# A planner that orders a decoder trunk's instructions: VectorE and GpSimd exclude each other in the plan, and the search over orders moves urgencies in one stretch of time

## The chip, the core and the metric

The kernel runs on one core of a Trainium2 chip. A core has TensorE (PE: matmuls; PEld in the profile is its weight load), VectorE (DVE), ScalarE (ACT), GpSimd (POOL) and SyncE (SP), which issues the DMAs here. Each engine works through its own list of instructions in order and waits at semaphores for the others. SBUF is the on-chip memory, PSUM holds what matmuls produce. The metric is the device time of one execution in microseconds (us).

## The reference

Two layers of a decoder over 528 positions (16 learned ones and 512 of the input) of width 1024, batch 1, all in float32. Each layer:

```python
xn = rmsnorm(h, norm_mix_g[l])
z_ret, z_hgrn, z_rwkv, z_s5 = split_cols(xn @ w_in[l], ...)
o_ret = retention_mixer(z_ret, pos)        # chunkwise retention with rotary positions
o_hgrn = hgrn2_mixer(z_hgrn, ...)          # gated linear recurrence
o_rwkv, v_first = rwkv7_mixer(z_rwkv, ...) # generalised delta rule, position by position
o_s5 = s5_mixer(z_s5, ...)                 # complex diagonal state space, associative scan
h = h + concatenate([o_ret, o_hgrn, o_rwkv, o_s5]) @ w_out[l]
hn = rmsnorm(h, norm_ffn_g[l])
h = h + square(relu(hn @ w_ffn_up[l])) @ w_ffn_down[l]   # 1024 -> 4096 -> 1024
```

A final rmsnorm follows, and the 512 positions of the input are returned.

## The kernel before, in words

Activations lie with features on the 128 partitions and positions along the free axis, in two halves of 272 and 256 columns (one of 512 in the last layer). A large product takes three matmuls: weights and activations are each split into a high and a low part (ScalarE rounds the high part `wh` from the raw weights `wr`, VectorE subtracts to get the low part `wl`), and high by high, high by low and low by high are summed in PSUM. These are the names `bpi` (input projection), `bpo` (output projection), `bpu` and `bpd` (MLP up and down). Weights come in 256 KB loads `wr` through SP's queue into three raw buffers.

The four mixers run as many small matmuls with work on VectorE, ScalarE and GpSimd between them, among the matmuls of the input projection and, at their end, of the output projection. In the S5 mixer two scans on VectorE give `Irs` and `Iis` (real and imaginary part); then `Xrs` is Irs times a table less `t2s`, and `t2s`, Iis times a table, is computed on GpSimd. In the retention mixer the rotary positions are a product on VectorE (`rkz` times `csr`), a product on GpSimd (`rksz` times `csr`), and their sum on VectorE. The chain of rwkv goes through three segments of 192 positions (`re`, `rm`, `rf`), with round trips through DRAM (`sa`, `sd`).

None of this order is written out by hand. The class `Sched` records every instruction (`record`, L108), prices it (`price`), and `flush` (L250) plans a whole stretch of the program: the first flush comes in the middle of layer 0's MLP, the second in the middle of layer 1's MLP, the third at the end. `run` (L138) is a list scheduler: it keeps a clock for each engine, takes at each step the engine that is free first, and of its ready instructions the one with the lowest key (its urgency). It models PSUM banks, the tiling of TensorE, SP's queue, and puts matmuls on zeros (named `z`, issued at L303) into waits of TensorE that it foresees, which keeps that engine active. On every other engine an instruction takes its price whatever the other engines do:

```python
            else:
                z=clk[e]=t+c
```

`flush` plans many times and keeps the order whose last instruction ends first by the plan. It starts from the program's order, goes back and forth through the graph for 10 turns, and then disturbs all keys of the best order so far with random numbers of spread 1 us, 30 times, with 3 plans each. The third flush has no such search. The best order is fixed by dependencies without semaphores between neighbours on an engine; all instructions are recorded under L304.

Of the kernel before, what the change touches and what calls it, by code (L numbers as in the profile page):

```python
# [6 lines left out]
T=528; NM=16; PADT=48; TP=576  # L7
# [39 lines left out]
    pass  # L47

# [1 line left out]
STEP=1; WARM=6500.0; LEAST=3500.0; SWITCH=.1; DRAIN=.05; KEEP=3.0; WCOLS=256; WCOST=.112; WSAFE=.4; FLB=2; NPRE=3; TURNS=10; SHAKES=30; SHAKE=1.0; BANKS=8; CLASS=dict(hv='a',rw='a',hg='a',mx='a'); OWN=dict(a=3)  # L50
class _Engine:

    def __init__(s,eng,name,sched): s.eng=eng; s.name=name; s.sched=sched
# [3 lines left out]
        return g  # L57

class _Op:
    __slots__=("e","op","f","a","k","deps","pre","cost","succ","ready","cols","nbytes","chain","label","pri","order","mode","at","opens","banks")  # L60

TICK=10.24/3
def _box(x):
# [14 lines left out]
def _meet(a,b):  # L78
    if a[0]>b[1] or b[0]>a[1]: return False
    if a[2] is None or b[2] is None: return True  # L80
    return all(p<=w and v<=q for (p,q),(v,w) in zip(a[2],b[2]))
# [6 lines left out]
class Sched:  # L88
# [19 lines left out]
    def record(s,e,op,f,a,k):  # L108
        o=_Op(); o.e=e; o.op=op; o.mode=o.at=None; o.f=f; o.a=a; o.k=k; o.succ=[]; o.cols=o.nbytes=0; o.ready=0.0; o.chain=None; o.label=s.label; o.pri=s.pri
        if s.pri is not None: s.pri+=1  # L110
        out=k["out"] if "out" in k else a[0]
        ins=[x for x in list(a)+list(k.values()) if hasattr(x,"tensor") and x is not out]
        n=1
        for d in out.shape[1:]: n*=d
        price(o,out,ins,n)
        i=len(s.ops); deps=set()
        if op=="matmul":
            t=(out.tensor.name,out.offset)
            if k.get("start"): s.first[t]=i
            else: o.chain=s.first.get(t)  # L120
        if op=="matmul" and not k.get("start") or op=="copy_predicated": ins.append(out)
        for x,w in [(y,0) for y in ins]+[(out,1)]:
            t=x.tensor.name
            b=(0,1<<40,((0,1<<40),)) if t in s.psum else _box(x)
            W=s.wr.setdefault(t,[]); R=s.rd.setdefault(t,[])
            for c,j in W:
                if j!=i and _meet(b,c): deps.add(j)
            if w:
                for c,j in R:
                    if j!=i and _meet(b,c): deps.add(j)  # L130
                s.wr[t]=[(c,j) for c,j in W if not _within(c,b)]+[(b,i)]
                s.rd[t]=[(c,j) for c,j in R if j==i or not _within(c,b)]
            else: R.append((b,i))
            u=s.users.setdefault(t,[])
            if not u or u[-1]!=i: u.append(i)
            o.ready=max(o.ready,s.done.get(t,0.0))
        o.deps=deps; o.order=s.after-deps; s.ops.append(o)
    def run(s,key,back=False):  # L138


        ops=s.ops; N=len(ops)
        clk={e:0.0 for e in s.clk} if back else dict(s.clk); hw,dma=(0.0,0.0) if back else s.queue; mode,place=s.tiling; recent=collections.deque(s.recent); act=sum(x for _,x in recent); idle=[None]*N
        ready={e:[] for e in clk}; late={e:[] for e in clk}
# [1 line left out]
        push=heapq.heappush; pop=heapq.heappop  # L145

        free=sorted(s.banks); due=[]; use=dict(s.count) if not back else {}; place_={}; spare=BANKS-sum(OWN.values()); own=dict.fromkeys(OWN,0); extra=0
        line={c:0 for c in OWN}; dirty={}
        def can(i,t):

            v=ops[i].opens
# [9 lines left out]
        while todo:  # L161
            t=1e18
            for x in clk:
                p=late[x]; r=ready[x]
                while p and p[0][0]<=clk[x]:
                    i=pop(p)[1]; push(r,(key[i],i))
# [7 lines left out]
            while p and p[0][0]<=t:  # L174
                i=pop(p)[1]; push(r,(key[i],i))
            if e=="tensor" and not back:
                while due and due[0][0]<=t:
                    z,b,c=pop(due); push(free,(z,b))
# [6 lines left out]
            else:  # L185


                x=min(r_)
# [3 lines left out]
                o=ops[x[1]]  # L192
# [4 lines left out]
                i=x[1]; o=ops[i]; c=o.cost  # L197

                if o.mode!=mode: c+=SWITCH+(DRAIN if place is not None else 0.0); dirty={}
                if o.opens is not None:  # L200
                    x=min((y for y in free if y[0]<=t and not (o.mode[0]<128 and y[1] in dirty)),default=None) or free[0]
# [6 lines left out]
                if s.idle is not None:  # L208
                    K,M=[max(x,64) for x in o.mode]; p=clk[e]; w=WCOLS*K/128.0; d=WCOST if K==M==128 else WCOST/2+.002; fill=[]
                    x=sorted(y for y in free if y[0]+WSAFE<=p)  # L210
                    if K==128: x=[y[1] for y in x[:1]]
                    else:
                        z=[[y[1] for y in x if y[1]%2==q] for q in (0,1)]
                        x=[z[0][0],z[1][0]] if z[0] and z[1] and len(x)>3 else []
# [15 lines left out]
                mode=o.mode; place=o.at  # L230
                recent.append((t,o.cols)); act+=o.cols
            T[i]=t
            if o.nbytes:
                clk[e]=t+.06
                if back: hw=max(hw,t)+max(o.cost,o.nbytes/360e3); z=hw+.65
                else: hw=max(hw,t)+o.cost; z=dma=max(dma,hw+(.784 if e=="scalar" else .65))+o.nbytes/360e3
            else:
                z=clk[e]=t+c
            Z[i]=z
            if not back:  # L240
                for v in o.banks:
# [8 lines left out]
    def flush(s,turns=0):  # L250
        ops=s.ops

        last={}
        for (pn,tag),(bufs,names) in s.tags.items(): last.setdefault(pn,[]).extend(names[-bufs:])
        for (pn,tag),(bufs,names) in s.tags.items():
            for q,t in enumerate(names):
                if t not in s.users: continue
                if q>=bufs: before=[names[q-bufs]]
                else: before=last.get(pn-1,[]) if isinstance(pn,int) else []
                mine=set(s.users[t]); old=set(i for x in before for i in s.users.get(x,[])); at=max([s.done.get(x,0.0) for x in before],default=0.0)  # L260
                for i in s.users[t]:
                    if not ops[i].deps&mine: ops[i].deps|=old; ops[i].ready=max(ops[i].ready,at)
        s.count={}; s.queue_={c:[] for c in OWN}; s.until={}
        for i,o in enumerate(ops):
            o.opens=None; o.banks=sorted({x.tensor.name for x in list(o.a)+list(o.k.values()) if hasattr(x,"tensor")}&s.psum)
            for v in o.banks:
                if v not in s.count: s.count[v]=0; o.opens=v; s.queue_[s.tag[v]].append(v)
                s.count[v]+=1
        for o in ops: o.pre=[(j,lat(ops[j],o)) for j in o.deps]+[(j,-1e9) for j in o.order]
        for i,o in enumerate(ops):  # L270
            for j,l in o.pre: ops[j].succ.append((i,l))
        chain=lambda x: [o.pri-1e9 if o.pri is not None else x[i if o.chain is None else o.chain] for i,o in enumerate(ops)]
        best=None; key=list(range(len(ops))); keys=[key]
        def attempt(key,n):
            nonlocal best
            for it in range(n):
                if it: key=chain([-z for z in s.run([-z for z in Z],True)[1]])
                T,Z,state=s.run(key); m=max(Z)
                if best is None or m<max(best[1]): best=T,Z,state; keys[0]=key
        attempt(key,1)  # L280
        if turns:
            best=None; attempt(chain([-z for z in s.run([-z for z in s.run(key)[1]],True)[1]]),turns)

            rnd=random.Random(1)
            for _ in range(SHAKES):
                m=max(best[1]); key=[x+rnd.gauss(0.0,SHAKE) for x in keys[0]]; attempt(chain(key),3)
        T,Z,(s.clk,s.queue,s.tiling,s.recent,s.banks,idle,where)=best
        for t in s.users: s.done[t]=max(Z[i] for i in s.users[t])
        real={}
        def ap(x):  # L290
            if not hasattr(x,"tensor") or x.tensor.name not in s.psum: return x
            n=x.tensor.name
            if n not in real:
                b=where[n][0]; real[n]=s.pool.tile([128,512],F32,name="b"+n,tag=f"b{b}",bufs=1).tensor; s.now[b]=n
            return bass.AP(real[n],x.offset,x.ap)
        def issue(e,x):
            if e in s.prev: s.tc.add_manual_dep(x.ins,s.prev[e].ins.name,mybir.DependencyInfo(mybir.DependencyClass.NoSync,mybir.DependencyReason.DATA),reason="order")
            s.prev[e]=x
        for t,i in sorted((t,i) for i,t in enumerate(T)):
            o=ops[i]  # L300
            for b,K,M,p,q in idle[i] or ():
                if not hasattr(s.now[b],"tensor"): s.now[b]=s.pool.tile([128,512],F32,name=f"z{b}",tag=f"b{b}",bufs=1)
                issue("tensor",s.nc.tensor.matmul(s.now[b][q:q+M,:WCOLS],s.idle[p:p+K,:M],s.idle[p:p+K,:WCOLS],start=True,stop=True))  # L303
            issue(o.e,o.f(*[ap(x) for x in o.a],**{k:ap(x) for k,x in o.k.items()}))  # L304
        s.start()
# [891 lines left out]
def build(tc,A,o_ap):  # L1197
# [4 lines left out]
    with tc.tile_pool(name="kp",bufs=1) as kp, tc.tile_pool(name="ps",bufs=1,space=bass.MemoryType.PSUM) as pp:  # L1202
# [13 lines left out]
        class Weights:  # L1216
# [20 lines left out]
            def take(s,n=2):  # L1237
                while s.n<s.at+3: s.ahead()
                j=s.at; s.at+=n
                return j  # L1240
        def heavy(w,xs,n0,n1,nm,m=128,order=range(8),step=STEP,last=False):

# [402 lines left out]
```

## Time and profile before

| what | us |
|---|---|
| median of 3 runs | 1519.39 |
| lowest and highest of the 3 | 1514.93, 1519.92 |
| profiled execution | 1513.31 |
| its span, first to last instruction | 1511.5 |

The profiled execution's time is 1.8 us more than its span. Busy time of an engine is the time in which at least one of its instructions runs. Matmuls overlap (a matmul of 272 columns is listed with some 0.29 us, and the next starts about 0.12 us later), so TensorE's busy time also covers moments in which it works below its rate. A wait is listed with the engine and tile that ended it.

### The profile page before, as it was taken

How to read it: one execution, taken by the hardware profiler on the slowest of the kernel's cores; microseconds unless marked ns; L12 is line 12 of the kernel's file. 1: busy time of each engine (PE TensorE's matmuls, PEld its weight loads, DVE VectorE, ACT ScalarE, POOL GpSimd, SP SyncE). 2: the span in 40 equal slices, each digit the busy share in tenths (PEclk: the TensorE clock that was granted, in tenths of full speed). 3: DMA queues.
4: the chain of work that ended last, by engine and by line, in shares of the span. 5: the costliest groups of instructions: out<-in, count | busy, mean ns of one | idle time of the engine just before them, and what ended most of it. 6: DMA issues, size and time to landing. Idle time of an engine off the chain costs nothing.

```text
span 1511.5 us, 30536 instructions
## 1 busy us (share of the span) xinstructions
PE 1468.0 (97%) x11696; PEld 1334.1 (88%) x11696; DVE 922.2 (61%) x2237; ACT 582.1 (39%) x1163; POOL 428.2 (28%) x577
## 2 busy tenths in 40 slices
PE   9999998999999999999999999988999999999998
PEld 8988898779999999999999988987788888888887
DVE  8967888797833338333656756887957333333345
ACT  4443324632632423324434424246325323232342
POOL 3512673443323235332001100233311222222210
PEclk9999999999999999999999999999999999999999
DMA  5542345422222224323446624455112332322332
GB/s 175 176 141 74 102 136 158 132 58 71 91 92 85 98 85 136 112 85 95 131 136 209 178 55 116 132 164 173 57 63 92 97 98 91 98 93 96 98 105 77
DMA packets 143298, 168.54 MB, mean 112 GB/s; under 512 B 52144, under 2 KB 77168, under 8 KB 143152
## 3 DMA queue, kind: packets, MB, share of 16 engines
q1 hardware_dynamic: 143152, 166.59, 36.1%
q8 instruction: 92, 1.51, 0.4%
q14 instruction: 54, 0.44, 0.1%
HBM read 138.65 MB, written 27.56 MB: 110 GB/s over the span
## 4 chain that ended last, share of the span: by engine, by line
PE 75%; DVE 11%; DMA 5%; issue 4%; ACT 2%; SPq 1%; POOL 1%; POOLq 0%; DVEq 0%; ACTq 0%
PE bpd_v L304 24%; PE bpu_v L304 23%; PE bpi_v L304 10%; PE bpo_v L304 6%; PE z L303 2%; DVE wl L304 1%; SPq L304 1%; DMA wr<-in_win 1%; POOL t2s L304 1%; DMA sa<-Gm_L1c 0%; DVE Irs L304 0%; DMA vfv01c<-zdv 0%; PE bpor0c_v L304 0%; DMA csr1c<-in_cs 0%; DVE tms L304 0%
## 5 line engine op out<-in xcount | busy, mean ns | idle before, releaser
L304 ACT ACTIVATE wh<-wr 128x512 fp32r<-128x512 f32 (+1 forms) x388 | 243.5, 628 | 545.3 <-PE bpd_v L304 220.9
L304 DVE TENSOR_TENSOR wl<-wr,wh 128x512 fp32r<-128x512 f32 (+1 forms) x388 | 269.1, 695 | 280.2 <-ACT wh L304 277.5
L304 PE MATMUL bpi_v<-xha,wh 128*128 128x272 f32 (+2 forms) x864 | 253.8, 295 | 1.1 <-DVE ht_L1c L304 0.9
L304 PE MATMUL bpi_v<-xha,wl 128*128 128x272 f32 (+2 forms) x864 | 248.8, 289 | 3.2 <-DVE wl L304 3.2
L304 PE MATMUL bpi_v<-xla,wh 128*128 128x272 f32 (+2 forms) x864 | 247.2, 287 | 0.0
L304 PE MATMUL bpu_v<-xhf,wl 128*128 128x272 f32 (+2 forms) x768 | 246.7, 321 | 0.5 <-DVE wl L304 0.5
L304 PE MATMUL bpu_v<-xhf,wh 128*128 128x272 f32 (+2 forms) x768 | 247.0, 322 | 0.0
L304 PE MATMUL bpu_v<-xlf,wh 128*128 128x272 f32 (+2 forms) x768 | 245.4, 320 | 0.0
L304 PE MATMUL bpd_v<-xhh,wh 128*128 128x256 f32 (+2 forms) x736 | 233.8, 318 | 0.0
L304 PE MATMUL bpd_v<-xhh,wl 128*128 128x272 f32 (+2 forms) x736 | 233.6, 318 | 0.0
L304 PE MATMUL bpd_v<-xlh,wh 128*128 128x256 f32 (+2 forms) x736 | 232.5, 317 | 0.0
L304 POOL TENSOR_TENSOR xlh<-fs,xhh 128x272 fp32r<-128x272 f32 (+2 forms) x96 | 94.3, 982 | 309.9 <-DVE fs L304 236.0
L304 PEld LDWEIGHTS bpi_v<-xha,wh 128*128 128x128 f32 (+1 forms) x864 | 161.3, 187 | 5.7 <-DVE ht_L1c L304 1.2
L304 PEld LDWEIGHTS bpi_v<-xha,wl 128*128 128x128 f32 (+1 forms) x864 | 160.9, 187 | 5.5 <-DVE wl L304 4.1
L304 PEld LDWEIGHTS bpi_v<-xla,wh 128*128 128x128 f32 (+1 forms) x864 | 161.0, 186 | 1.0 <-issue 0.3
L304 PEld LDWEIGHTS bpu_v<-xhf,wl 128*128 128x128 f32 x768 | 144.5, 188 | 12.0 <-DVE wl L304 0.7
L304 PEld LDWEIGHTS bpu_v<-xlf,wh 128*128 128x128 f32 x768 | 144.5, 188 | 11.4
L304 PEld LDWEIGHTS bpu_v<-xhf,wh 128*128 128x128 f32 x768 | 144.6, 188 | 10.7
L304 PEld LDWEIGHTS bpd_v<-xlh,wh 128*128 128x128 f32 x736 | 138.3, 188 | 10.0
L304 PEld LDWEIGHTS bpd_v<-xhh,wl 128*128 128x128 f32 x736 | 138.3, 188 | 9.9
L304 PEld LDWEIGHTS bpd_v<-xhh,wh 128*128 128x128 f32 x736 | 138.4, 188 | 9.3
L304 POOL TENSOR_TENSOR h<-h,fd 128x272 f32<-128x272 f32 (+2 forms) x72 | 86.9, 1207 | 184.7 <-DVE fd L304 184.7
(922 smaller groups left out, 2534.3 us busy)
## 6 DMA issues: line engine op xcount, KB each, us to landing
wr<-in_wup SPq DMA_DIRECT2D x128, 256.0 KB
wr<-in_wdn SPq DMA_DIRECT2D x128, 256.0 KB
wr<-in_win SPq DMA_DIRECT2D x104, 256.0 KB
wr<-in_wout SPq DMA_DIRECT2D x32, 256.0 KB
h<-in_x SPq DMA_DIRECT2D x16, 264.0 KB
hD<-h SPq DMA_DIRECT2D x8, 264.0 KB
h<-hD SPq DMA_DIRECT2D x8, 264.0 KB
out<-out SPq DMA_DIRECT2D x8, 256.0 KB
```

The costliest lines, as they stand in the source:

```text
L303: issue("tensor",s.nc.tensor.matmul(s.now[b][q:q+M,:WCOLS],s.idle[p:p+K,:M],s.idle[p:p+K,:WCOLS],start=True,stop=True))
L304: issue(o.e,o.f(*[ap(x) for x in o.a],**{k:ap(x) for k,x in o.k.items()}))
```

## The change

Three things. `record` marks each instruction that uses the path shared by VectorE and GpSimd (`port`): every GpSimd instruction but memset; on VectorE those with two inputs in SBUF, and tensor_scalar and copies with an input in SBUF. `run` keeps three times in `held`: the end of VectorE's last marked instruction, and start and end of GpSimd's hold. A marked VectorE instruction that would start within GpSimd's hold starts at the hold's end. A marked GpSimd instruction has 0.33 us of its own (POOLUP), then takes the path at the end of VectorE's marked instruction. And `flush` makes 150 attempts in place of 30: the first 30 as before, 120 more with one plan each, in which only keys of instructions that start within one random stretch of 10 to 120 us are disturbed, by a spread of 0.3, 1 or 3 us; half of them start from keys taken from the plan backwards.

```diff
-STEP=1; WARM=6500.0; LEAST=3500.0; SWITCH=.1; DRAIN=.05; KEEP=3.0; WCOLS=256; WCOST=.112; WSAFE=.4; FLB=2; NPRE=3; TURNS=10; SHAKES=30; SHAKE=1.0; BANKS=8; CLASS=dict(hv='a',rw='a',hg='a',mx='a'); OWN=dict(a=3)
+STEP=1; WARM=6500.0; LEAST=3500.0; SWITCH=.1; DRAIN=.05; KEEP=3.0; WCOLS=256; WCOST=.112; WSAFE=.4; FLB=2; NPRE=3; TURNS=10; SHAKES=150; SHAKE=1.0; BANKS=8; POOLUP=.33; CLASS=dict(hv='a',rw='a',hg='a',mx='a'); OWN=dict(a=3)
...
         price(o,out,ins,n)
+
+        sb=sum(str(x.space).endswith("SB") for x in ins)
+        o.port=e=="gpsimd" and op!="memset" or e=="vector" and (sb>1 or sb and op in ("tensor_scalar","tensor_copy"))
...
-        line={c:0 for c in OWN}; dirty={}
+        line={c:0 for c in OWN}; dirty={}; held=[0.0]*3
...
             else:
-                z=clk[e]=t+c
+                if not o.port or back: z=t+c
+                elif e=="vector": z=held[0]=(held[2] if held[1]<=t<held[2] else t)+c
+                else: x=min(POOLUP,c); held[1]=max(t+x,held[0]); z=held[2]=held[1]+c-x
+                clk[e]=z
...
             rnd=random.Random(1)
-            for _ in range(SHAKES):
-                m=max(best[1]); key=[x+rnd.gauss(0.0,SHAKE) for x in keys[0]]; attempt(chain(key),3)
+            for it in range(SHAKES):
+                if it<30: key=[x+rnd.gauss(0.0,SHAKE) for x in keys[0]]; attempt(chain(key),3); continue
+                T,Z,_=best; m=max(Z); w=rnd.uniform(10.0,120.0); a=rnd.uniform(min(T)-w,m); d=rnd.choice((.3,1.0,3.0)); k=keys[0]
+                if rnd.random()<.5: k=chain([-z for z in s.run([-z for z in Z],True)[1]])
+                attempt([x+rnd.gauss(0.0,d) if a<=T[i]<=a+w and ops[i].pri is None else x for i,x in enumerate(k)],1)
```

The lists of instructions change order on every engine in the first two flushes. In the changed program the helper's lines are L312 (matmuls on zeros) and L313. Three lists follow, from two places.

VectorE, layer 0, second half of S5 (`01` in the names), before: the scans, then Irs and Xis times their table, the low part of a weight tile (`wl52`), a product of hgrn (`Kh0c0`), and the update of Xrs with GpSimd's t2s.

```order
L304 TENSOR_TENSOR Xrs01_626<-Irs01_621,Ps01_618 128x4x132
L304 SCALAR_TENSOR_TENSOR Iis01_622<-s5m4_370,Jis01_624 128x132
L304 TENSOR_TENSOR Irs01_621<-Irs01_621,Ps01_618 128x528
L304 TENSOR_TENSOR Xis01_627<-Iis01_622,Ps01_618 128x4x132
L304 COPY_PREDICATED hA160_526<-cst_62,blv1h0c0_v178_4239 16x32
L304 TENSOR_TENSOR wl52_321<-wr52_315,wh52_320 128x512
L304 TENSOR_TENSOR Kh0c0_534<-Kh0c0_534,tth0c0_537 128x4x4
L304 TENSOR_TENSOR Xrs01_626<-Xrs01_626,t2s01_628 128x4x132
```

The same place of the changed program.

```order
L313 TENSOR_TENSOR Xrs01_626<-Irs01_621,Ps01_618 128x4x132
L313 SCALAR_TENSOR_TENSOR Iis01_622<-s5m4_370,Jis01_624 128x132 x2
L313 TENSOR_TENSOR Irs01_621<-Irs01_621,Ps01_618 128x528
L313 TENSOR_TENSOR Xis01_627<-Iis01_622,Ps01_618 128x4x132
L313 TENSOR_TENSOR Xrs01_626<-Xrs01_626,t2s01_628 128x4x132
```

The weight tile's low part and the hgrn product no longer stand between Xis and the update of Xrs.

TensorE at the same place, before: the end of a projection (`bpi0_50`), a level of hgrn (`blv4`), then S5's output (`bs5y0s01`, of whose three matmuls for a group the one from Us needs no scan).

```order
L304 MATMUL bpi0_50_128_272_v54_4309<-xla7_95,wh51_317 128x256
L304 MATMUL bpi0_50_128_272_v54_4309<-xha7_94,wl51_318 128x256
L304 MATMUL blv4h0c0_v181_4344<-hB160_527,Kh0c0_534 16x16 x2
L304 MATMUL bs5y0s01_v229_4249<-Xrs01_626,CTs01_613 128x132
L304 MATMUL bs5y0s01_v229_4249<-Xis01_627,CTs01_613 128x132
```

The same place of the changed program.

```order
L313 MATMUL bpi0_50_128_272_v54_4331<-xla7_95,wh51_317 128x256
L313 MATMUL bpi0_50_128_272_v54_4331<-xha7_94,wl51_318 128x256
L313 MATMUL bs5y0s01_v229_4386<-Us01_620,M1s01_615 128x132
L313 MATMUL bs5y2s01_v230_4389<-Us01_620,M1s01_615 128x132
L313 MATMUL bpi0_52_128_0_v55_4393<-xha0_80,wh52_320 128x272
L313 MATMUL bpi0_52_128_0_v55_4393<-xla0_81,wh52_320 128x272
L313 MATMUL bs5y0s01_v229_4386<-Xrs01_626,CTs01_613 128x132
```

Two matmuls from Us and two of the next projection now stand ahead of the first use of Xrs.

TensorE in layer 1, at the transposes `btmkr1c1` of the retention keys `rkz`, before: behind a bonus term of rwkv, hgrn's diagonal and first level (`blv1`), with fills.

```order
L304 MATMUL bpb1L1c6_v616_15041<-bo_L1c6_8956,cst_62 128x192
L304 MATMUL bdgh1c2_v657_15044<-cst_62,QKh1c2_9022 128x2
L304 MATMUL blv1h1c2_v656_15048<-hB1281_8987,Kh1c2_9020 128x128 x2
L303 LDWEIGHTS zero_65
L303 MATMUL z2_15052<-zero_65 128x256
L303 LDWEIGHTS zero_65
L303 MATMUL z2_15052<-zero_65 128x256
L304 MATMUL blv1h1c2_v656_15048<-hB1281_8987,Kh1c2_9020 128x128
L304 MATMUL btmkr1c1_v696_15058<-cst_62,rkz1c1_9080 128x128 x3
```

The same place of the changed program.

```order
L313 MATMUL blv1h1c2_v656_15080<-hB1281_9007,Kh1c2_9040 128x128 x4
L313 MATMUL bzp2L1c6_v632_15089<-tav_L1c6_8979,tbk_L1c6_8980 64x64
L313 MATMUL bpo12L1c6_v634_15093<-SL1c0_8897,rav_L1c6_8967 64x64
L313 MATMUL bpo02L1c6_v633_15096<-SL1c0_8897,rav_L1c6_8967 64x64
L313 MATMUL bpo12L1c6_v634_15093<-tav_L1c6_8979,Gm_L1c6_8971 64x64
L313 MATMUL bpo02L1c6_v633_15096<-tav_L1c6_8979,Gm_L1c6_8971 64x64
L313 MATMUL bpo02L1c6_v633_15096<-SL1c0_8897,rav_L1c6_8967 64x64
L313 MATMUL bpo12L1c6_v634_15093<-SL1c0_8897,rav_L1c6_8967 64x64
L313 MATMUL bpo02L1c6_v633_15096<-tav_L1c6_8979,Gm_L1c6_8971 64x64
L313 MATMUL bpo12L1c6_v634_15093<-tav_L1c6_8979,Gm_L1c6_8971 64x64
L313 MATMUL bzp2L1c6_v632_15089<-tav_L1c6_8979,tbk_L1c6_8980 64x64 x3
L313 MATMUL btmkr1c1_v696_15115<-cst_62,rkz1c1_9100 128x128 x4
```

Twelve small matmuls of the rwkv chain now stand between hgrn's first level and the transposes.

## Rows read from the trace of the kernel before

**Rows 1.** The page: span, engines' busy time, share, instructions.
```profile
span 1511.5 us, 30536 instructions
...
PE 1468.0 (97%) x11696; PEld 1334.1 (88%) x11696; DVE 922.2 (61%) x2237; ACT 582.1 (39%) x1163; POOL 428.2 (28%) x577
...
```

**Rows 2.** Windows of five stages: length, busy us (instructions) by engine, granted clock, DMA.
```profile
...
0.00:350.00 350.00, 331.46 (x3290) 301.14 (x3291) 286.68 (x852) 147.56 (x323) 145.60 (x259) 0.99 0.43 125
350.00:786.00 436.00, 435.53 (x3591) 435.06 (x3590) 222.54 (x511) 164.02 (x317) 125.53 (x159) 1.00 0.32 102
786.00:1100.00 314.00, 296.90 (x2946) 266.38 (x2945) 230.78 (x577) 127.47 (x279) 66.74 (x94) 0.99 0.45 134
1100.00:1491.00 391.00, 390.90 (x1768) 319.37 (x1768) 170.62 (x269) 140.75 (x240) 88.91 (x63) 1.00 0.29 92
...
```

**Rows 3.** The same windows, the fill matmuls z alone.
```profile
...
0.00:350.00 350.00, 35.76 (x240) 0.99 0.43 125
...
786.00:1100.00 314.00, 27.94 (x180) 0.99 0.45 134
...
```

**Rows 4.** Page, group of the fill matmuls: busy us, mean ns, idle before.
```profile
L303 PE MATMUL z<-zero 128*128 128x256 bf16 (+3 forms) x462 | 69.1, 291 | 1.1 <-POOL zero L304 1.1
```

**Rows 5.** Waits of PE: us in total, times, longest.
```profile
...
PE bs5y0s_v L304 <- DVE Xrs L304: 3.6, 3, 2.1
...
PE btmkr0c_v L304 <- DVE rkz0c L304: 2.6, 2, 1.9
...
PE btmkr1c_v L304 <- DVE rkz1c L304: 2.4, 2, 1.4
...
```

**Rows 6.** GpSimd by form: busy us, mean ns, idle before.
```profile
...
L304 POOL TENSOR_TENSOR t2s<-Iis,Ps 128x528 f32<-128x528 f32 x4 | 10.4, 2594 | 4.0 <-DVE Iis L304 4.0
...
L304 POOL TENSOR_TENSOR tts<-Iis,Ps 128x528 f32<-128x528 f32 x4 | 6.2, 1556 | 14.1 <-ACT Iis L304 14.1
...
```

**Rows 7.** Timeline around 237 us: start, us, engine, instruction, idle before.
```profile
...
236.62 0.68 DVE L304 TENSOR_TENSOR Irs<-Irs,Ps 128x528 f32<-128x528 f32 x1
...
236.84 2.93 POOL L304 TENSOR_TENSOR t2s<-Iis,Ps 128x528 f32<-128x528 f32 x1 [1.25 <-DVE Iis L304]
...
237.22 0.69 DVE L304 TENSOR_TENSOR Xis<-Iis,Ps 128x528 f32<-128x528 f32 x1
...
237.94 0.67 DVE L304 TENSOR_TENSOR wl<-wr,wh 128x512 fp32r<-128x512 f32 x1
...
238.54 1.26 DVE L304 TENSOR_TENSOR Kh0c<-Kh0c,tth0c 128x16 f32<-128x16 f32 x1
...
240.57 0.49 PE L304 MATMUL bs5y0s_v<-Xrs,CTs 128*128 128x132 f32 x2 [2.12 <-DVE Xrs L304]
...
```

**Rows 8.** Timeline around 1055 us.
```profile
...
1053.01 1.56 POOL L304 TENSOR_TENSOR rksz1c<-rksz1c,csr1c 128x512 f32<-128x512 f32 x1 [1.98 <-DVE rqz1c L304]
...
1053.60 1.52 DVE L304 TENSOR_TENSOR rkz1c<-rkz1c,csr1c 128x512 f32<-128x512 f32 x1
...
1056.93 0.52 PE L304 MATMUL btmkr1c_v<-cst,rkz1c 128*128 128x128 f32 x3 [1.40 <-DVE rkz1c L304]
...
```

**Rows 9.** Chain of waits, 0 to 390 us: start, us, what.
```profile
...
329.44 1.68 DVE rqz0c L304
332.61 1.40 DVE rqz0c L304
...
```

**Rows 10.** Chain of waits, 786 to 1145 us.
```profile
...
814.34 6.11 DMA wr<-in_win
...
967.36 2.87 POOL t2s L304
...
1083.78 1.49 DVE rqz1c L304
...
```

**Rows 11.** Waits of SP's queue.
```profile
...
SPq L304 <- DVE wl L304: 655.8, 255, 15.0
...
```

**Rows 12.** Windows, one stretch of 50 us with a lower granted clock.
```profile
...
850.00:900.00 50.00, 48.42 (x560) 41.24 (x559) 31.70 (x89) 18.48 (x44) 6.69 (x12) 0.97 0.29 82
...
```

More of the change, by code (lines that the diff above doesn't have):

```diff
@@ L59 @@
 class _Op:
-    __slots__=("e","op","f","a","k","deps","pre","cost","succ","ready","cols","nbytes","chain","label","pri","order","mode","at","opens","banks")
+    __slots__=("e","op","f","a","k","deps","pre","cost","succ","ready","cols","nbytes","chain","label","pri","order","mode","at","opens","banks","port")
 TICK=10.24/3
```

## The prediction

> **What bounds the kernel now.** I read the page's busy times first, then busy time by stage, then who waits for whom, then the timeline at the longest waits. TensorE is busy for 1468.0 of the span's 1511.5 us [rows 1]. By stage [rows 2] it is full in both MLP stages, which with the output projections take 350 to 786 and 1100 to 1491 us: 435.53 of 436 us and 390.90 of 391 us. No order of VectorE or GpSimd can shorten those. What can move lies in the two mixer stages, 0 to 350 and 786 to 1100 us: 18.5 us (350 - 331.46) and 17.1 us (314 - 296.90) without a matmul, 35.6 us in all, and 35.8 + 27.9 = 63.7 us of matmuls on zeros that the planner put into waits which it foresaw [rows 3]. So each mixer stage is planned waits (filled), unplanned waits (empty), and work that stays.
>
> Of the empty waits several end in a VectorE instruction that shares its inputs' path with GpSimd: TensorE waits 3.6 us in 3 times for Xrs, and 2.6 and 2.4 us for the two rkz [rows 5]. Behind them two engines hold each other up. The product t2s on GpSimd takes 2594 ns on average, the same product of the same shape, tts, 1556 ns [rows 6]. At 236.84 us t2s starts while VectorE runs Irs, and ends 2.93 us later; VectorE's Xis and wl, which start after it, take their usual 0.69 and 0.67 us, and then Kh0c, a product of only 128x16, takes 1.26 us; TensorE has waited 2.12 us for Xrs when it goes on at 240.57 us [rows 7]. At 1053 us it is the other way round: rksz on GpSimd takes 1.56 us, VectorE's rkz, 128x512, takes 1.52 us where wl of that size took 0.67 us, and TensorE waits 1.40 us for what follows [rows 7, 8]. The old planner knows nothing of this.
>
> **The change part by part.** No instruction that computes is added, removed or resized. Each engine's list holds the same instructions; only the matmuls on zeros go from 462 to 469. So the sum consists of waits.
>
> *The planner charges the exclusion.* What it can win: the four t2s take 10.4 us where four tts take 6.2 us, 4.2 us too many [rows 6], and t2s stands on the chain of waits [rows 10]. On the chain there are five rotary products of 128x512 that are stretched in the same way (1.68, 1.40, 1.48, 1.57, 1.49 us; first two and last in [rows 9, 10]): 7.62 us against 5 x 0.67 us, 4.3 us too many. Together 8.5 us on the path. A planner cannot abolish the exclusion, both instructions have to run; it can put other matmuls in the gap, or take away what VectorE runs in between. The orders shown in the section on the change do both. In layer 0 wl and Kh0c no longer stand between Xis and the update of Xrs. That lets t2s in 0.67 us earlier (wl, [rows 7]; Kh0c only waited along with it), and four matmuls that need no Xrs stand ahead of TensorE's first use of it, 0.12 us each by the full stage (435.53 us for 3591, [rows 2]): 1.2 of the 2.12 us. In layer 1 twelve small matmuls of the rwkv chain now come between the first hgrn products and the transpose that waited 1.40 us, so that most of this wait is covered. Elsewhere the order shows nothing so plain. I take half, 4.2 us, with 0 and 8.5 us as ends.
>
> *The search goes on.* The 30 disturbed orders of before stay, and 120 more follow, each moving the urgencies in one stretch. Nothing in this trace shows what one more try brings. From below it is nothing, or a loss where the plan is wrong; from above it is all the empty time that the first term left, 35.6 - 4.2 us, and the fills besides. The nearest row is that of the fills, since they are what a planner sees as waiting: 63.7 us in the two stages [rows 3]. I take a twelfth of it, 5 us, as a choice and not a measurement.
>
> *Seven more fills.* The group of 462 costs 69.1 us [rows 4], 0.15 us each: 1.0 us more of time that the plan itself calls waiting. That the new plan foresees about as much waiting as the old one, although it now charges an exclusion that the old one left out, is the best sign that the order as such is better; had the count gone up by 50 I would forecast no gain.
>
> *The rest.* The last stage (second half of the last MLP and the final norm) is planned without a search in both versions, and its fills stand where they stood; 0. The clock: the granted clock of TensorE is 0.97 in four windows of 50 us, as at 850 us [rows 12], and 1.00 in nearly all others; each such window costs 0.03 x 50 = 1.5 us. Fills that stand elsewhere can add or spare one; 0, with 1.5 us to either side. The computing of the plan is not on the chip; 0.
>
> Sum: 4.2 + 5 - 1.0 = 8.2 us. The profiled execution took 1513.3 us, so 1505.1 us for one like it. The median of the three runs shown is 1519.4 us, 6.1 us above it, with the lowest at 1514.9; on that level the sum gives 1511 us, which is my forecast.
>
> **Rivals.** *The planner hands the shared path to the wrong engine; the time stays.* Its rule lets a GpSimd instruction in as soon as VectorE's running instruction ends, and makes VectorE's next one wait. In [rows 7] two more VectorE instructions, Xis and wl, went first, each started before the one ahead had ended, and t2s came only after. By the planner's rule t2s would have been done some 0.69 + 0.67 = 1.4 us earlier. Where matmuls were placed by the promised time, the wait comes back: in all four new orders Irs and Xis still run side by side with t2s. Then the first term falls to about 1 us and the search, which optimises on the same wrong promise, to about 2 us: 1519.4 - 2 = 1517 us. Against it: both instructions must run before Xrs, so that the promise for Xrs itself is nearly right whichever goes first. The Trainium skill ("SBUF — State Buffer", section "Who interferes with whom") says that a VectorE instruction with two SBUF inputs contends with a GpSimd instruction that reads SBUF, and that whoever issues first blocks the other for the whole instruction. By that rule Xis at 237.22 us should have waited for t2s; the trace differs, Xis took its usual 0.69 us, and Kh0c alone waited.
>
> *Slower: weight loads come late.* All loads go through SP's queue in order, and that queue waits 655.8 us in 255 times for wl on VectorE [rows 11], since a raw weight buffer is free only when wl has read it. A plan that puts wl later to let GpSimd in delays the next load. In the chain one such load of 6.11 us stands at 814.34 us [rows 10]. If two more fall out of their cover in the mixer stages, that is +12 us against a gain of 4 us: about 1527 us. It decides where a wl is put off by more than the time that the projection matmuls in hand last. For it: three weight buffers are all there is. Against it: the planner models the queue and those buffers, and the last of the projections moves from matmul 7533 to 7647 in layer 1 (matmuls on zeros not counted), so there is more of them left to cover waits, not less.
>
> *A gain twice as large.* The exclusion is fully avoided (8.5 us) and the search earns 10 us: 1519.4 - 17.5 = 1502 us. For it speaks that 63.7 + 35.6 us of waiting are there; against it, that this order is already the best of a hundred tries.
>
> **How the numbers follow.** Forecast 0.41 (1504 to 1514 us), larger gain 0.19, no change 0.25, late loads or another loss of that kind 0.15. A difference under 0.3% (4.6 us) can't be told from none with this kernel. So faster 0.60, same 0.25, slower 0.15. The range reaches from somewhat beyond the larger gain to half of the slower case: 1495 to 1523 us.
>
> **What would show it.** Right: TensorE's waits for Xrs and rkz fall from 8.6 us (3.6 + 2.6 + 2.4, [rows 5]) to under 5 us; TensorE's empty time in the mixer stages falls from 35.6 to about 28 us; the MLP stages keep their 436 and 391 us within 1 us apart from where they begin; t2s still takes over 2.3 us on average, since Irs and Xis stay beside it. Wrong: the first MLP matmuls begin no earlier than before; new waits of TensorE on wl or on weight loads; more windows below 1.00 of the clock; or empty time that fell in one stage and came back as much in the other.

## The result and the profile after

The changed kernel is slower: 1528.86 us median of 12 executions against 1519.89, ratio 1.0057 [1.0035, 1.0079]. The forecast was 1511 us and its range ended at 1523. The execution profiled took 1530.77 us.

The page of the changed kernel, against [rows 1], and the group of its fills, against [rows 4]: TensorE is busy 22.5 us longer with the same real matmuls, and the fills are as many as the plan said.

```profile
span 1529.0 us, 30534 instructions
...
PE 1490.5 (97%) x11703; PEld 1351.5 (88%) x11703; DVE 918.7 (60%) x2237; ACT 582.1 (38%) x1163; POOL 422.6 (28%) x577
...
L312 PE MATMUL z<-zero 128*128 128x256 bf16 (+2 forms) x469 | 70.1, 298 | 1.1 <-POOL ones L313 1.1
```

Windows of the changed kernel, cut where its stages now end, against [rows 2]; columns as there.

```profile
0.00:360.00 360.00, 343.15 (x3356) 311.57 (x3357) 283.99 (x860) 148.85 (x325) 143.17 (x260) 0.97 0.43 123
360.00:800.00 440.00, 439.70 (x3628) 438.97 (x3627) 227.96 (x537) 166.32 (x322) 122.06 (x161) 1.00 0.33 104
800.00:1115.00 315.00, 301.00 (x2835) 267.88 (x2834) 223.31 (x541) 122.80 (x269) 66.22 (x92) 0.92 0.45 128
1115.00:1508.00 393.00, 393.00 (x1780) 320.50 (x1778) 171.89 (x270) 141.80 (x241) 89.75 (x63) 1.00 0.29 92
```

Both MLP stages are full as before. The first MLP matmul of layer 0 comes at 392.8 us where it came at 387.9, and layer 1 takes 386.2 us from the last matmul of the MLP before it to its own first MLP matmul, where it took 375.1. The mixers' empty time fell, 16.85 + 14.00 = 30.9 us where it was 35.6, and yet these stages end later: inside them TensorE was busy longer, at a granted clock of 0.97 and 0.92 instead of 0.99. Two stretches of 50 us, the first against [rows 12]:

```profile
850.00:900.00 50.00, 49.51 (x514) 42.69 (x513) 27.25 (x75) 19.17 (x45) 3.45 (x9) 0.86 0.39 109
1050.00:1100.00 50.00, 46.59 (x405) 38.26 (x405) 38.90 (x90) 22.11 (x50) 17.95 (x21) 0.83 0.36 102
```

Waits of TensorE in the changed kernel, the longest seven and three further down, against [rows 5]:

```profile
PE bs5y0s_v L313 <- DVE Xrs L313: 3.5, 2, 2.1
PE bpyL1c_v L313 <- DMA Em_L1c<-sd: 3.0, 1, 3.0
PE btmkh0c_v L313 <- DVE nvh0c L313: 2.3, 1, 2.3
PE blv4h0c_v L313 <- DVE hqz0c L313: 1.8, 1, 1.8
PE btmkr0c_v L313 <- DVE nxrw2L0c L313: 1.6, 1, 1.6
PE bhsL1c_v L313 <- DVE zps L313: 1.5, 1, 1.5
PE blv8h0c_v L313 <- ACT tvh0c L313: 1.5, 1, 1.5
...
PE btmkr0c_v L313 <- DVE rkz0c L313: 0.5, 1, 0.5
PE brs00r1c_v L313 <- DVE rkz1c L313: 0.5, 1, 0.5
...
PE bpi_v L313 <- DVE wl L313: 0.3, 1, 0.3
```

The waits for rkz are nearly gone (5.0 to 1.0 us), those for Xrs are not, and six that do not appear in the list of the kernel before take 11.7 us together. The kernel before had a wait for wl that the changed one hardly has:

```profile
PE bpi_v L304 <- DVE wl L304: 3.2, 4, 1.3
```

The timeline at S5's second half in layer 0, against [rows 7]:

```profile
237.07 0.68 DVE L313 TENSOR_TENSOR Irs<-Irs,Ps 128x528 f32<-128x528 f32 x1
237.23 2.30 POOL L313 TENSOR_TENSOR t2s<-Iis,Ps 128x528 f32<-128x528 f32 x1 [1.51 <-DVE Iis L313]
...
237.67 0.70 DVE L313 TENSOR_TENSOR Xis<-Iis,Ps 128x528 f32<-128x528 f32 x1
...
239.56 0.71 DVE L313 TENSOR_TENSOR Xrs<-Xrs,t2s 128x528 f32<-128x528 f32 x1 [1.19 <-POOL Xis L313]
...
240.32 0.49 PE L313 MATMUL bs5y0s_v<-Xrs,CTs 128*128 128x132 f32 x2 [2.07 <-DVE Xrs L313]
```

t2s takes 2.30 instead of 2.93 us since wl and Kh0c no longer run beside it: 0.63 us, where the prediction had 0.67. TensorE still waits as long (2.07 for 2.12 us): it comes to this point 1.02 us after t2s has begun (240.32 - 2.07 - 237.23), before 1.61 us after. And Xis starts 0.44 us after t2s and takes its usual 0.70 us. The changed plan had it the other way round: Xis held back, 1.60 us with its wait, and t2s undisturbed, 1.45 us.

GpSimd's products by form, against [rows 6]: t2s is stretched as before (10.3 for 10.4 us), and tts now too (8.6 for 6.2).

```profile
L313 POOL TENSOR_TENSOR t2s<-Iis,Ps 128x528 f32<-128x528 f32 x4 | 10.3, 2576 | 4.3 <-DVE Iis L313 4.3
...
L313 POOL TENSOR_TENSOR tts<-Iis,Ps 128x528 f32<-128x528 f32 x4 | 8.6, 2150 | 21.3 <-ACT Iis L313 21.3
```

The chain of waits from 780 to 1160 us, against [rows 10]. The weight load on it is short now; a t2s and a rotary product are still there, and a round trip of rwkv through DRAM (Em) takes 7.96 us:

```profile
827.39 2.22 DMA wr<-in_win
...
1010.75 2.88 POOL t2s L313
...
1030.14 7.96 DMA Em_L1c<-sd
...
1100.49 1.22 DVE rkz1c L313
```

SP's queue, against [rows 11]: in sum it waits as long for wl as before.

```profile
SPq L313 <- DVE wl L313: 656.6, 253, 15.0
```

### The profile page after: what moved, and what is told of

The parts are those of the page before. It is cut to its first block, busy times and chain, and to the rows that moved or that the text cites. A ratio compares the mean times of both kernels' runs of the same rounds, so it can differ in the third digit from the quotient of the medians.

```text
span 1529.0 us, 30534 instructions
## 1 busy us (share of the span) xinstructions
PE 1490.5 (97%) x11703; PEld 1351.5 (88%) x11703; DVE 918.7 (60%) x2237; ACT 582.1 (38%) x1163; POOL 422.6 (28%) x577
## 4 chain that ended last, share of the span: by engine, by line
PE 86%; DVE 5%; DMA 3%; issue 2%; ACT 2%; POOL 1%; SPq 1%; POOLq 0%; DVEq 0%; ACTq 0%
PE bpu_v L313 24%; PE bpd_v L313 23%; PE bpi_v L313 17%; PE bpo_v L313 5%; PE z L312 3%; SPq L313 1%; PE bs5g_v L313 1%; DMA Em_L1c<-sd 1%; PE bs5y0s_v L313 0%; PE bs5y2s_v L313 0%; PE bpoh1c_v L313 0%; PE bpor0c_v L313 0%; DVE wl L313 0%; PE bpor1c_v L313 0%; DMA zdrg<-zprg 0%
## 5 line engine op out<-in xcount | busy, mean ns | idle before, releaser
L313 ACT ACTIVATE wh<-wr 128x512 fp32r<-128x512 f32 (+1 forms) x388 | 243.1, 628 | 560.0 <-PE bpd_v L313 213.3
L313 DVE TENSOR_TENSOR wl<-wr,wh 128x512 fp32r<-128x512 f32 (+1 forms) x388 | 275.4, 712 | 298.1 <-ACT wh L313 282.9
L313 PE MATMUL bpi_v<-xha,wh 128*128 128x256 f32 (+2 forms) x864 | 254.8, 296 | 0.3 <-DVE zps L313 0.3
L313 PE MATMUL bpi_v<-xha,wl 128*128 128x256 f32 (+2 forms) x864 | 249.6, 290 | 0.3 <-DVE wl L313 0.3
L313 PE MATMUL bpi_v<-xla,wh 128*128 128x272 f32 (+2 forms) x864 | 249.4, 290 | 0.0
L313 PE MATMUL bpu_v<-xhf,wl 128*128 128x272 f32 (+2 forms) x768 | 246.1, 322 | 0.0
L313 PE MATMUL bpu_v<-xhf,wh 128*128 128x272 f32 (+2 forms) x768 | 245.9, 321 | 0.0
L313 PE MATMUL bpu_v<-xlf,wh 128*128 128x272 f32 (+2 forms) x768 | 245.4, 321 | 0.0
L313 PE MATMUL bpd_v<-xhh,wh 128*128 128x272 f32 (+2 forms) x736 | 232.6, 319 | 0.0
L313 PE MATMUL bpd_v<-xhh,wl 128*128 128x272 f32 (+2 forms) x736 | 232.5, 318 | 0.0
L313 PE MATMUL bpd_v<-xlh,wh 128*128 128x272 f32 (+2 forms) x736 | 231.9, 317 | 0.0
L313 POOL TENSOR_TENSOR xlh<-fs,xhh 128x272 fp32r<-128x272 f32 (+2 forms) x96 | 92.2, 963 | 301.0 <-DVE fs L313 216.7
L313 PEld LDWEIGHTS bpi_v<-xha,wh 128*128 128x128 f32 (+1 forms) x864 | 162.4, 188 | 4.5 <-issue 1.9
L313 PEld LDWEIGHTS bpi_v<-xha,wl 128*128 128x128 f32 (+1 forms) x864 | 162.3, 188 | 2.5 <-DVE wl L313 0.5
L313 PEld LDWEIGHTS bpi_v<-xla,wh 128*128 128x128 f32 (+1 forms) x864 | 162.6, 188 | 1.6 <-issue 0.2
L313 PEld LDWEIGHTS bpu_v<-xhf,wh 128*128 128x128 f32 x768 | 144.7, 189 | 11.7 <-ACT wh L313 0.2
L313 PEld LDWEIGHTS bpu_v<-xlf,wh 128*128 128x128 f32 x768 | 144.3, 188 | 11.3
L313 PEld LDWEIGHTS bpu_v<-xhf,wl 128*128 128x128 f32 x768 | 144.0, 188 | 11.0
L313 PEld LDWEIGHTS bpd_v<-xlh,wh 128*128 128x128 f32 x736 | 138.1, 188 | 10.0
L313 PEld LDWEIGHTS bpd_v<-xhh,wl 128*128 128x128 f32 x736 | 138.1, 188 | 9.9
L313 PEld LDWEIGHTS bpd_v<-xhh,wh 128*128 128x128 f32 x736 | 137.9, 188 | 9.6 <-ACT wh L313 0.2
L313 POOL TENSOR_TENSOR h<-h,fd 128x272 f32<-128x272 f32 (+2 forms) x72 | 85.9, 1195 | 189.3 <-DVE fd L313 187.5
```

## The experiments

Ratios are against the kernel before, timed on the same chip; medians of the kernel before were 1519.2 to 1521.7 us.

**The parts apart.** In the expectations theory A blames the clock, B the rule. The first kernel has the rule and 30 tries, the second 150 tries and no rule; both are edits of the changed kernel, the first cut to the one constant of its line.

```diff
-STEP=1; ... SHAKES=150; ...
+STEP=1; ... SHAKES=30; ...
```
```diff
-        o.port=e=="gpsimd" and op!="memset" or e=="vector" and (sb>1 or sb and op in ("tensor_scalar","tensor_copy"))
+        o.port=False
```

> The exclusion rule alone, with the 30 tries of before. Prediction's sum: 4.2 us less than before, 1515 to 1517 us. Theory B: this part carries the loss, 1525 us or more, and the waits on VectorE are longer than before. Theory A: the time follows the clock that this order happens to get: about 1515 us plus half of what it runs at 1.2 GHz beyond 22 us.

> The 120 local tries alone, without the exclusion rule. Prediction's sum: 5 us less than before, 1513 to 1516 us. Theory B: 1513 to 1517 us, since the wrong rule is gone. Theory A: about 1514 us plus half of what it runs at 1.2 GHz beyond 22 us.

Rule alone: 1528.51 us, 1.0042 [1.0014, 1.0069]. Tries alone: 1518.63 us, 0.9987 [0.9960, 1.0014]. On this seed the rule carries the loss, and the tries neither won nor lost anything clear of noise; B and the prediction had looked for less than 1518.63 from them. The granted clock of the rule alone was 0.985 in the median, as that of the kernel before; the clock of a median execution does not separate these two. Theory A's sums, from the time at 1.2 GHz by the clock's records of each profile, are 1515 + (44.8 - 22)/2 = 1526 us for the rule, near what it took, and 1514 + (61.4 - 22)/2 = 1534 us for the tries, 15 us too much. In its profile, with a span of 1522.6 us, TensorE with the rule alone is busy 12.6 us longer than in [rows 1], and its fills take 8.7 us more, 529 where [rows 4] has 462:

```profile
PE 1480.6 (97%) x11763; PEld 1346.7 (88%) x11763; DVE 921.4 (61%) x2237; ACT 581.2 (38%) x1163; POOL 421.6 (28%) x577
...
L312 PE MATMUL z<-zero 128*128 128x256 bf16 (+3 forms) x529 | 77.8, 289 | 1.7 <-POOL ones L313 1.1 <-ACT tvh1c L313 0.4
```

**More filling.** A table adds fills in front of the TensorE instructions that waited in the mixers; no other instruction moves. The lines that add them, without the table and its counter:

```diff
...
+                    x=x or (mine if o.opens is not None and K==128 else [])
+                    if x and more and (K==128 or fill):
+                        j=len(fill); fill=fill+[(x[q%len(x)],K,M,K*(q%len(x)),M*(q//len(x)%(128//M))) for q in range(j,j+more)]
...
```

> The changed kernel with its order and plan untouched (no real instruction stands elsewhere on any engine) and 404 more filling matmuls on zeros, put by a table in front of the TensorE instructions of the mixer stages that waited over 0.25 us in the changed kernel's profile: some 45 us of filling into 54 us of waits. Theory A (the new order is no longer than the old one; TensorE ran 74.6 us at 1.2 GHz instead of 21.7 us because its unforeseen waits stood unfilled): the pieces at 1.2 GHz fall under 30 us, the mean granted clock goes from 0.976 to 0.99 or above, and the time falls by 12 to 26 us, to 1503 to 1517 us. Theory B (the new order itself is later: a wrong price of the exclusion hands the shared path to the wrong engine): the clock may rise, but the time stays at 1526 to 1532 us, or goes up with the filling.

> The same done to the kernel before: order and plan untouched, 483 more filling matmuls in front of the instructions that waited in its profile (59 us of waits). It has only 21.7 us at 1.2 GHz, 13.6 us of them in the mixer stages. Theory A: at most some 7 us to win, so 1512 to 1520 us, and the changed kernel with its filling is faster than this one by the 5 to 9 us that the plan foresaw. Theory B: this one stays the fastest, at 1515 to 1525 us, 5 us or more below the changed kernel with filling. If filling as such costs time: over 1525 us.

The changed kernel with more fills: 1538.52 us, 1.0117 [1.0074, 1.0161], at a granted clock of 0.994. The kernel before with more fills: 1532.44 us, 1.0070 [1.0046, 1.0094], at 0.994. The clock rose in both and both became slower, so theory A's remedy fails. It does not measure what the clock costs, since much of the filling missed its wait. The timeline of the padded changed kernel at one of the places:

```profile
312.81 0.50 PE L319 MATMUL blv8h0c_v<-hB,Kh0c 128*128 128x128 f32 x3
314.88 1.91 PE L318 MATMUL z<-zero 128*128 128x256 bf16 x16 [1.57 <-DVE nxrw2L0c L319]
316.85 0.66 PE L319 MATMUL btmkr0c_v<-cst,rkz0c 128*128 128x128 f32 x4
```

In the changed kernel btmkr0c waited 1.57 us for the same nxrw2L0c, at 311.39 us. The fills write to the PSUM bank that it opens, wait for that bank's reader as it did, and then delay it by 1.91 us. Nor must a lower clock mean a longer time. A kernel of a later group, the one before on a third seed, whose windows

```profile
0.00:360.00 360.00, 345.16 (x3373) 314.61 (x3374) 289.61 (x865) 150.07 (x328) 148.92 (x268) 0.98 0.43 124
800.00:1115.00 315.00, 299.45 (x2923) 267.59 (x2923) 229.13 (x541) 123.97 (x277) 70.24 (x97) 0.96 0.44 128
```

have the clock at 0.98 and 0.96; by the clock's records it ran 48.1 us at 1.2 GHz (the kernel before 21.7, the changed one 74.6), and its span is 1512.1 us, as short as that of the kernel before. It is another order, so this is no price of the clock; it does show that time at 1.2 GHz alone does not rank the orders.

**The halves of the rule.** Both with 30 tries: one kernel lets only GpSimd wait, the other only holds VectorE; each on seeds 1 and 3. Theory V blames VectorE's half, G GpSimd's, W is V with the wrong engine named, M says that any other order is slower on average.

```diff
-                elif e=="vector": z=held[0]=(held[2] if held[1]<=t<held[2] else t)+c
+                elif e=="vector": z=held[0]=t+c
```
```diff
-                else: x=min(POOLUP,c); held[1]=max(t+x,held[0]); z=held[2]=held[1]+c-x
+                else: x=min(POOLUP,c); held[1]=t+x; z=held[2]=t+c
```

> The exclusion rule's GpSimd half alone, with the 30 tries of before: a GpSimd instruction waits for the end of VectorE's running one, VectorE is never held. Theory V (the loss is VectorE's charge: the plan of the rule holds VectorE back 50 us in 126 places, where the trace shows VectorE's instructions stretched by 33 us in all with the rule or without it): 1516 to 1523 us, no slower than before. Theory G (the loss is GpSimd's: its price holds the stretch already, 393 us of price against 398 measured, and the rule adds 24 us): 1525 us or more, like the full rule alone (1528.5).

> The rule's VectorE half alone, 30 tries: VectorE is held while GpSimd runs beyond its first 0.33 us, GpSimd takes its old price and waits for nothing. Theory V: 1525 us or more, the whole loss of the full rule. Theory G: 1517 to 1523 us, like before.

> The GpSimd half of the rule alone on seed 3, where the kernel without the rule took 1514.6 us and the full rule 1528.7. Theory W (the plan hands the shared path to the wrong engine: in the changed kernel it holds 82 VectorE instructions back by 53.5 us, and the trace shows only 22 of them stretched, by 13.2 us; what it lets GpSimd wait, 113.5 us planned against 112.4 measured, is right): 1513 to 1520 us. Theory M (leaving an order that was the best of many draws costs, whatever is changed): 1520 to 1535 us, as on seed 1 (1538.8).

> The VectorE half of the rule alone on seed 3. Theory W: 1525 to 1533 us, the whole loss. Theory M: 1518 to 1535 us, and no nearer to the full rule than the other half is.

GpSimd's half: 1538.79 us (1.0115 [1.0080, 1.0150]) on seed 1, 1523.33 (1.0027 [0.9998, 1.0057]) on seed 3. VectorE's half: 1536.50 (1.0102 [1.0072, 1.0131]) and 1527.67 (1.0059 [1.0035, 1.0082]). On seed 1 each half alone is slower than both together, which neither V nor G nor W allows; on seed 3 W missed for GpSimd's half (1513 to 1520 us) and held for VectorE's. M's ranges held, but not its clause that VectorE's half is no nearer to the full rule (1528.65): it is, by 1.0 us against 5.3. Neither half carries the loss on both seeds.

**Other seeds.** The only edit; without the rule seeds 2 to 5, with the rule alone (30 tries) seeds 2 to 5. Theory L is a lottery, S says that the seed of the kernel before is an outlier, R that the rule's price makes orders worse.

```diff
-            rnd=random.Random(1)
+            rnd=random.Random(3)
```

> The full rule with the 30 tries of before, drawn from another random seed. Theory V or G (the rule costs): 1525 to 1532 us again. Theory L (a lottery: any other order of this planner lies some us to either side): anywhere from 1515 to 1535 us, and more than 4 us away from the 1528.5 us of the first seed.

> The kernel before with another random seed and nothing else. By its own plan this order is 7 us longer than that of the first seed. Theories V and G: the plan without the rule ranks its own orders rightly, so about 1525 to 1530 us. Theory L: anywhere from 1513 to 1535 us, with no relation to the plan's 7 us.

> The kernel before with a third random seed and nothing else. Theory S (selection: the seed of the kernel before happens to be an outlier; its own plan ends at 1458.0 us, those of five other seeds at 1462.7 to 1465.8; a change of the planner throws this draw away): 1526 to 1538 us, like the second seed (1536). Theory R (the rule's price makes orders worse, the second seed was bad luck): 1516 to 1524 us.

> The exclusion rule alone with the 30 tries of before and a third random seed. Theory S: 1526 to 1535 us, the rule's orders lie no higher than the orders of other seeds without it. Theory R: 1526 to 1535 us too, but then 5 us or more above what seeds 3 and 4 give without the rule.

> The kernel before with a fourth seed. Its plan ends at 1463.7 us. Theory S: 1526 to 1538 us. Theory R: 1516 to 1524 us.

> The rule alone with a fourth seed; its plan ends at 1480.6 us, the lowest of the rule's first four seeds (1482.0, 1481.9, 1482.6). Theory S: 1524 to 1534 us, and the mean of the rule's four seeds within 3 us of the mean of the four without it. Theory R: the rule's mean is 5 us or more above.

> The kernel before with a fifth random seed; its plan ends at 1463.0 us. If the rule costs some 7 us on average: 1515 to 1528 us, and 3 us or more below the rule's order of this seed. If the six pairs were luck: no lower than the rule's order.

> The rule alone on the fifth seed, 30 tries; its plan ends at 1480.9 us. The rule's four other seeds lie close together (1528.5 to 1534.4 us): 1526 to 1535 us if they are a sample of what the rule gives. If the rule costs: 3 us or more above the same seed without it.

| seed | no rule: us, ratio | plan's end | rule alone: us, ratio | plan's end |
|---|---|---|---|---|
| 1 | 1520.28, 1 (the kernel before, 129 executions) | 1458.0 | 1528.51, 1.0042 [1.0014, 1.0069] | 1482.0 |
| 2 | 1536.09, 1.0101 [1.0059, 1.0143] | 1465.0 | 1532.31, 1.0081 [1.0055, 1.0107] | 1481.9 |
| 3 | 1514.65, 0.9962 [0.9941, 0.9984] | 1462.7 | 1528.65, 1.0063 [1.0037, 1.0090] | 1482.6 |
| 4 | 1522.65, 1.0010 [0.9987, 1.0033] | 1463.7 | 1534.43, 1.0099 [1.0071, 1.0128] | 1480.6 |
| 5 | 1529.17, 1.0063 [1.0039, 1.0088] | 1463.0 | 1524.23, 1.0011 [0.9985, 1.0037] | 1480.9 |

A random seed alone moves the time by 21 us, more than the change did. S falls with seeds 3 and 4; R, as a rule for every seed, with seeds 2 and 5, where the rule is the faster side. What is left is L, though not by its letter: 1536.09 lies 1 us beyond its range for seed 2, and 1532.31 not quite 4 us from the first seed. The rule's fifth seed lies 2 us under the 1526 to 1535 us expected of it. The plan's own end does not rank the draws: 1463.0 gave 1529, 1462.7 gave 1515.

**The tries on another seed.** The two kernels with 150 tries, on seed 3.

> No rule, seed 3, with the 120 local tries: the candidate to beat both kernels. On seed 1 these tries took 2 us off (1520.5 to 1518.6). By theory W the plan without the rule is ranked rightly enough that its own gain of 3.0 us (1462.7 to 1459.7) shows: 1509 to 1514 us. By theory M: 1512 to 1522 us, a gain of the plan means nothing at this size.

> The whole change on seed 3 (rule and 120 local tries). The plan gains 8.9 us by the tries over the rule alone (1482.6 to 1473.7). Theory W: the tries work on wrong prices, so 1524 to 1531 us, no real gain over 1528.7. Prediction's view of the search (5 us): 1521 to 1525 us. Theory M: 1518 to 1535 us.

Without the rule 1519.58 us, 1.0003 [0.9982, 1.0024]; with it, the whole change on seed 3, 1521.10 us, 1.0005 [0.9973, 1.0038]. The tries took 7.6 us off the rule's order (1528.65) and put 4.9 us on the other (1514.65), by medians of different groups. W missed both; M held both, and the prediction's view of the search held for the second (1521 to 1525 us), where on seed 1 the same tries took nothing off the rule's order (1528.51 to 1528.86). The fastest kernel of all is the one before with seed 3 and no part of the change; the interval leaves it 0.2 to 0.6% ahead.

## Why the prediction was wrong

**The failed step is the first term, "The planner charges the exclusion": 4.2 us, with 0 as its lower end.** On this seed the rule alone cost 0.42% (6.4 us) where a gain of 4.2 stood. The local working held in part: t2s is done 0.63 us sooner after its start, and the waits for Xrs and rkz fell from 8.6 to 4.5 us (under 5 was forecast). At the S5 place itself nothing was won: the earlier t2s and four matmuls were to take 1.2 us off TensorE's wait, which is 2.07 us where it was 2.12. (Two of the five rotary products on the chain, at 332.61 and 1055.23 us, are the sums of the products; they are stretched like them.) What failed is the step from these places to the sum, and the premise under it that the old order stays otherwise. A new price moves every list in two flushes; other waits take 11.7 us, so that the empty time fell by 4.7 us only, and TensorE's busy time rose by 22.5 us in the profiles shown, by 12.6 us with the rule alone. The sum priced an edit, and the change was also a new draw.

How draws fall is shown: seventeen other orders of this planner (seeds, halves, rule, tries, the changed kernel itself) have ratios from 0.9962 to 1.0115, with a mean of 1.0046. Two lie below 1, one of them clearly. The kernel before is a good draw among these, the changed kernel's 1.0057 an ordinary one. The mean is 7 us, but eleven of the seventeen carry the rule or a half of it, with a mean of 1.0060; the six without have 1.0021, which is not clear of 1. The prediction had this in one clause, as an argument against a larger gain (the order is already the best of a hundred tries); it is an argument for a loss as well, and the spread, some 20 us, belonged in the range.

Whether the rule itself costs, beyond the draw, stays open. In seven pairs that differ by the rule alone (five seeds, and seeds 1 and 3 with 150 tries) it cost 0.42, -0.20, 1.01, 0.89, -0.52, 0.70 and 0.02%: mean 0.33%, 95% interval -0.21 to 0.87%. So it also stays open how much of the 6.4 us on this seed is the rule's price and how much the draw.

**The first rival's mechanism is there, and its price was wrong.** Laid beside the trace instruction by instruction, the changed plan holds 82 VectorE instructions back by over 0.2 us, 53.5 us in all; in the trace 22 of them are stretched by that much, 13.2 us. The 88 GpSimd instructions that it makes wait by over 0.1 us take 112.4 us, planned 113.5. So at the places that the plan names VectorE mostly goes ahead and GpSimd pays. VectorE pays too, but elsewhere: the expectation of the GpSimd half alone counts 33 us by which VectorE's instructions are stretched in all, with the rule or without. The rule follows what the Trainium skill states ("SBUF — State Buffer", section "Who interferes with whom"), that whoever issues first blocks the other for the whole instruction; the trace disagrees, with Xis at 0.70 us inside t2s. Still the rule brings the plan's end nearer: with 30 tries the spans profiled end 40 to 47 us after the plan's end with it, 49 to 64 us without. A plan with a nearer end was no faster one, and taking VectorE's half out did not help on seed 1.

**The search.** 5 us was a choice from the fills. Without the rule the tries shorten the plan by 0.4 us on seed 1 and 3.0 on seed 3, and measured -0.13% [-0.40, 0.14] and, beside the same seed, +4.9 us. With the rule they shorten the plan by 6.6 us on seed 1 (1482.0 to 1475.4) and 8.9 on seed 3, and the medians changed by +0.4 and -7.6 us. A gain in the plan is no measure of one on the chip; the fills, which are what the plan sees, were the wrong row to size it by.

**The fills.** 469 and 70.1 us, as forecast. But the prediction took the small count as the best sign for the order, and 50 more as a sign of no gain. The rule alone has 529, 67 more than before, and by that sign no gain was to be expected of it; the tries brought the count back down, not the time.

**The clock.** "0, with 1.5 us to either side" was read from one execution. Over the 129 executions of the kernel before that were timed beside the experiments the granted clock runs from 0.975 to 0.993, median 0.985: the profile shown stands at the top of that range, and that of the changed kernel has the lowest of its 12 (0.976 to 0.986, median 0.981). Side by side these two profiles make the clock look like the whole loss, 53 us more at 1.2 GHz, which was theory A; the medians differ by 0.004. Within the 129 executions a clock lower by 0.009 goes with 8.1 us more (last section), so an estimate is that some 4 of the 9 us go with the clock. Whether it is their cause is open, and the rule alone lost its 6.4 us at the same clock.

**The rest.** The MLP stages kept their times: from first to last matmul 378.3 and 360.7 us where it was 379.5 and 357.9, and 1.9 us of the last are matmuls of the output projection that now stand in between. Late weight loads do not show (SP's queue waits 656.6 us for wl against 655.8, TensorE 0.3 against 3.2, the load on the chain takes 2.22 instead of 6.11 us), so the slower rival was right only in its sign. Setting the forecast at the level of the median, not of the profiled execution, was right.

## What to carry to other kernels

Where a change re-plans a whole program, its effect is that of the edit plus that of leaving the present draw; time a few seeds on both sides before crediting or blaming the edit, and keep the spread between seeds in the range. A gain shown at three places of the new order says little about the sum, since every other place of the order is new as well. Compare two profiles only after placing each among its kernel's other executions, by time and by clock.

## What the runs showed of the hardware

Within one program time and granted clock go together: of the kernel before, 20 executions at 0.989 or above have a median of 1515.9 us, 21 at 0.980 to 0.982 one of 1524.0. That is no proof that the clock makes the time: longer waits may lower the clock as well. Raising it by fills did not bring the time along (0.994 and 1532 to 1539 us), but the fills took time of their own. And VectorE's Xis, with two inputs in SBUF, ran at its usual length beside a GpSimd product that had begun, which then took 2.30 us where its like takes 1.56 in [rows 6]. It is not always VectorE that goes ahead: in [rows 7] Kh0c took 1.26 us beside the end of such a product.
